# Every fourth raw weight block of the first layer in a fourth buffer, in the room of the third output-map buffer

## The chip, the cores and the metric

The kernel runs on one core of a Trainium2 chip. The metric is the device time of one execution in microseconds (us). Before the change three runs gave a median of 934.77 us (934.74 to 936.48). A core has five engines with queues of their own: TensorE (PE) multiplies matrices into PSUM banks, VectorE (DVE), ScalarE (ACT) and GpSimd (POOL) work elementwise, and SyncE (SP) issues DMA transfers. Each engine takes its instructions in the order in which they were put into its queue; semaphores order the engines against each other.

## The reference

Two layers over a sequence of 512 tokens of width 1024. The first layer projects the normalised input into five parts of 1024 columns; one part feeds a state-space branch, two feed a convolution branch, and two are gates. The second layer is a gated linear attention.

```python
u = rms_norm(x, norm_pre[i])
p = u @ ev_w_in[j]
a_in, a_z, b_val, b_gate, b_z = split(p)          # 1024 columns each
ya = s5_layer(a_in, ...)                          # 64 groups of 16 channels, state of 64
ya = gelu(ya)
ya = ya * sigmoid(ya @ s5_w_glu[j] + s5_b_glu[j]) * silu(a_z)
yb = conformer_conv(b_val, b_gate, ...) * silu(b_z)   # causal width 31, layer norm, projection
y = concatenate([ya, yb]) @ ev_w_out[j]
x = x + rms_norm(y, norm_post[i])
...
# second layer: the same frame around chunked gated linear attention
```

In `s5_layer` every group runs s_t = Lbar s_(t-1) + Bbar u_t and gives y_t = Re(C s_t) + D u_t.

## The kernel before

All products are made in a split precision: a weight block of 128 x 1024 is loaded raw (tile `wraw`), ScalarE rounds it to a high half `wh` (L155), and a low half `wl` = raw - high is made beside it. One output tile of 128 x 512 then takes 24 matmuls: 8 of high weight by high input (L198), 8 of high weight by low input (L199) and 8 of low weight by high input (L201).

The weight blocks form one list in order of use. Blocks 0 to 7 of `ev_w_in` give the input of the state-space branch; blocks 8 to 39 come in eight rounds of four (convolution value, convolution gate, and the two gates); blocks 40 to 47 are `s5_w_glu`; the rest follows. `w_raw` allocates the next raw tile and lets SP issue its load (L118). The tiles rotate through three buffers of one pool on the left side of the on-chip memory. `w_split` makes the halves; for blocks 0 to 47 the low half is made by ACT (L130: minus the raw block, rounded) and a DMA that POOL issues and that adds the raw block to it (L131). So a raw buffer comes free when both L155 and the landing of L131 are done. After each split `w_raw` is called once, so that in the program's order the raw loads run two blocks ahead of the split.

The state-space branch works on eight chunks c of 128 channels, each in three generator functions whose steps are interleaved with the projection blocks:

- `s5_prep(c)` loads the coefficients `cb` (L534; three buffers), makes the input map `bmt`/`bm` (L548, L550, L552 on DVE for the first two chunks, on POOL for the others), the direct kernel `kt` (PE L571 and L575, a copy `ks` on ACT L574, DVE L577), which goes through DRAM into the tile `tm` (L584, L586), and the output map `cme` of 128 x 1024 (the same lines L548, L550, L552, always on DVE, with the scratch tile `pt`). `phases(c)` on POOL (L522 to L524) makes rotation tables that are loaded into `ct` and `st` (L594).
- `s5_in(c)` loads the re-ordered input `u` (L605), multiplies it by `bm` (PE L609), rotates, scans and rotates back (L621 to L636).
- `s5_out(c)` multiplies `u` by `tm` and the states `sv` by `cme` (PE L649), copies and transposes (L653, L658), and applies the gelu into `ya` (ACT L664).

A round c runs `s5_in(c + 1)`, `s5_prep(c + 2)` and `s5_out(c)` in alternating steps and then the four blocks: `value_gate(c)` (sigmoid on ACT L700, product on DVE L701, and the convolution of 31 taps on DVE, L673 to L677, at the lowest priority) and `gate_z` twice (ACT L714, store by SP L715).

The tiles of the state-space branch lie in two pools on the right side, `q5` and `h5`, which are opened after the parameters are computed and closed after the last round; the tiles of the next stage (among them `sz`, `yah`, `yal`, `yfh`, `yfl`) then take this room, each as soon as the tiles that lay there are done with. `cme` has three buffers there, `bm`, `tm` and `kt` two.

The order on each engine isn't written out: a list scheduler puts the instructions into the queues by priority and by the times of its own model, and gives a tile its buffer when one is free in that model. `feed()` raises a priority, `background()` lowers it. A change of a buffer count so can move instructions of any queue.

After round 7 come the GLU product (blocks 40 to 47), the layer norm of the convolution output (`ln`, `xbh`, `xbl`), the output projections, and the second layer.

Of the kernel before, what the change touches and what calls it, by code (L numbers as in the profile page):

```python
# [9 lines left out]
F32 = mybir.dt.float32  # L10
# [7 lines left out]
P = 128  # L18
# [7 lines left out]
GP = 16  # L26
NS = 64
GC = P // GP
NB = 64
DVE_PREP = 2  # L30
TB = S // NB
# [20 lines left out]
def trunk(ctx: ExitStack, tc: tile.TileContext, A: dict, out: bass.AP, dbg: dict | None = None):  # L52
# [6 lines left out]
    wpool = ctx.enter_context(tc.tile_pool(name="wpool", bufs=2, side="left"))  # L59
# [4 lines left out]
    def dump(name, ap):  # L64
        if name in dbg:
            SY.dma_start(dbg[name], ap)
# [3 lines left out]
    def ps(tag="mm"):  # L70
        n = banks["bufs"][tag]
        return banks["pool"].tile([P, S], F32, tag=tag, bufs=n, name=f"ps_{tag}")

    def tmp(shape=(P, S), dt=F32, name="tmp"):
        return t2.tile(list(shape), dt, tag="t2", name=name)
# [35 lines left out]
    wst = {"next_raw": 0, "next_split": 0, "raw": {}, "hl": {}, "low": {}}  # L111

    def w_raw():
        i = wst["next_raw"]
        if i >= len(wlist):
            return
        raw = wpool.tile([P, 1024], F32, tag="wraw", bufs=3, name=f"wraw{i}")
        SY.dma_start(raw, wlist[i][1] if isinstance(wlist[i], tuple) else wlist[i])  # L118
        wst["raw"][i] = raw
        wst["next_raw"] = i + 1  # L120

    def w_low(i, dst=None):


        while wst["next_raw"] <= i:
            w_raw()
        l = wpool.tile([P, 1024], F32R, tag="wl", bufs=3, name=f"wl{i}") if dst is None else dst
        raw = wst["raw"][i]
        with feed():
            SC.activation(l, raw, AF.Copy, scale=-1.0)  # L130
            G.dma_start(l.bitcast(F32), raw, accum_op=ALU.add)  # L131
        wst["low"][i] = l

    def w_split(dst=None):
        i = wst["next_split"]
        while wst["next_raw"] <= i:
            w_raw()
# [4 lines left out]
        if isinstance(wlist[i], tuple):  # L142

            l = wpool.tile([P, 1024], F32R, tag="wl", bufs=3, name=f"wl{i}") if dst is None else dst[1]
            for e in range(2):
                es_, g_ = slice(e * S, (e + 1) * S), wst["gain"][:, 2 * wlist[i][0] + e:2 * wlist[i][0] + e + 1]
                with feed():
                    SC.activation(h[:, es_], raw[:, es_], AF.Copy, scale=g_)  # L148
                    V.scalar_tensor_tensor(out=l[:, es_], in0=raw[:, es_], scalar=g_, in1=h[:, es_].bitcast(F32), op0=ALU.mult, op1=ALU.subtract)  # L149
            wst["hl"][i] = (h, l)  # L150
            wst["next_split"] = i + 1
            w_raw()
            return
# [14 lines left out]
    def feed():  # L168
        return tc.high_priority(offset=1500)
# [310 lines left out]
    q5 = S5.enter_context(tc.tile_pool(name="q5", bufs=1, side="right", reuse_waits="tile"))  # L480
    h5 = S5.enter_context(tc.tile_pool(name="h5", bufs=2, side="right", reuse_waits="tile"))

    dump("u0h", uh.bitcast(F32))


# [21 lines left out]
    def phases(c):  # L507

        sh = [P, GC, 8, 8]
        ws = slice(c // 2 * GC, c // 2 * GC + GC)  # L510

        def w1(w):
            return wb[:, 1, w, ws, :].unsqueeze(3).to_broadcast(sh)

        def w0(w):
            return wb[:, 0, w, ws, :].unsqueeze(2).to_broadcast(sh)

        out_ = []
        for o, (a, b, op) in enumerate(((0, 1, ALU.subtract), (1, 0, ALU.add))):
            r_ = h5.tile(sh, F32, tag=f"ph{o}", bufs=1, name=f"ph{o}_{c}")  # L520
            wt = h5.tile(sh, F32, tag="wt", bufs=1, name=f"wt{o}_{c}")
            G.tensor_tensor(out=r_, in0=w1(0), in1=w0(a), op=ALU.mult)  # L522
            G.tensor_tensor(out=wt, in0=w1(1), in1=w0(b), op=ALU.mult)
            G.tensor_tensor(out=r_, in0=r_, in1=wt, op=op)  # L524
            out_.append(r_.rearrange("p g a b -> p (g a b)"))
        pair[c // 2] = out_
# [3 lines left out]
    def coefficients(c):  # L530

        if c < KT:
            cbs[c] = h5.tile([P, 4, GC, GP], F32, tag="cb", bufs=3, name=f"cb{c}")
            SY.dma_start(cbs[c], A["s5cb"][c])  # L534

    def s5_prep(c):

        g0_ = c * GC
        pe_ = V if c < DVE_PREP else G
        gs = slice(g0_, g0_ + GC)  # L540
        cb = cbs.pop(c)
        cr_ = csps[c % 2]
        SC.activation(cr_[:, :, 0:GP], cb[:, 0], AF.Copy, scale=sgn)

        def outer(eng, o, pt, h, pw, m1, m2, pa):
            sh = list(o.shape)
            hg = slice(g0_ + h * 4, g0_ + h * 4 + 4)
            eng.tensor_tensor(out=o, in0=pw[:, 0, hg, 0:TB].unsqueeze(pa).to_broadcast(sh),  # L548
                              in1=m1.unsqueeze(5 - pa).to_broadcast(sh), op=ALU.mult)
            eng.tensor_tensor(out=pt, in0=pw[:, 1, hg, 0:TB].unsqueeze(pa).to_broadcast(sh),  # L550
                              in1=m2.unsqueeze(5 - pa).to_broadcast(sh), op=ALU.mult)
            eng.tensor_tensor(out=o, in0=o, in1=pt, op=ALU.add)  # L552

        bm = q5.tile([P, GC, P], F32, tag="bm", bufs=2, name=f"bm{c}")
        cme = q5.tile([P, GC, TB, GP], F32, tag="cme", bufs=3, name=f"cme{c}")
        kt = q5.tile([P, GC, GP], F32, tag="kt", bufs=2, name=f"kt{c}")
        for h in range(2):
            hs = slice(h * 4, h * 4 + 4)
            bmt = q5.tile([P, 4, GP, TB], F32, tag="bmt", bufs=2, name=f"bmt{c}")
            pt1 = h5.tile([P, 4, GP, TB], F32, tag="wt", bufs=1, name=f"pt1_{c}")  # L560
            outer(pe_, bmt, pt1, h, prb, cb[:, 2, hs], cb[:, 3, hs], 2)
            tp = ps("aux")
            for j in range(4):
                PE.transpose(tp[:, j * P:(j + 1) * P], bmt[:, j].rearrange("p q s -> p (q s)"), ident)
            with feed():
                SC.copy(bm[:, hs, :], tp.rearrange("p (g n) -> p g n", n=P))
            yield

            kp = ps("aux")
            for j in range(4):  # L570
                PE.matmul(kp[32 * j:32 * j + 32, 0:P], cr_[:, h * 4 + j, :], bmt[:, j].rearrange("p q s -> p (q s)"), start=True, stop=True)  # L571
            ks = q5.tile([P, P], F32, tag="ks", bufs=2, name=f"ks{c}")
            with feed():
                SC.copy(ks, kp[:, 0:P])  # L574
            PE.transpose(kp[:, P:2 * P], ks, ident)  # L575
            with feed():
                V.tensor_tensor(out=kt[:, hs, :], in0=kp[:, P:2 * P].rearrange("p (g q) -> p g q", q=32)[:, :, 0:GP],  # L577
                                in1=dg[:, g0_ + h * 4:g0_ + h * 4 + 4, :], op=ALU.add)
            pt2 = q5.tile([P, 4, TB, GP], F32, tag="pt", bufs=1, name=f"pt2_{c}")
            outer(V, cme[:, hs], pt2, h, pr, cb[:, 0, hs], cb[:, 1, hs], 3)  # L580
            yield
        coefficients(c + 3)
        kd = kt_d[c % 2]
        SY.dma_start(kd[:, 0:TB], kt.rearrange("p g q -> p (g q)"))  # L584
        tm = q5.tile([P, TB, GC, GP], F32, tag="tm", bufs=2, name=f"tm{c}")
        SY.dma_start(tm, bass.AP(tensor=kd.tensor, offset=kd.offset, ap=[[(2 * TB - 1) * P, GP], [P, TB], [1, TB * P]]))  # L586

        if c % 2 == 0:
            phases(c)
        half = slice(c % 2 * NS, c % 2 * NS + NS)  # L590
        ct_, st_ = (h5.tile([P, S], F32, tag=n, bufs=2, name=f"{n}{c}") for n in ("ct", "st"))
        for dst, src in zip((ct_, st_), pair[c // 2]):
            for r_ in range(2):
                SY.dma_start(dst[r_ * NS:r_ * NS + NS], src[half])  # L594
        prep[c] = (bm, cme, tm, ct_, st_)
        yield
# [126 lines left out]
    for c in range(2):  # L723
        run(s5_prep(c), 5)
    run(s5_in(0), 2)
    for c in range(KT):
        nx = s5_in(c + 1) if c + 1 < KT else iter([None] * 2)
        pre = s5_prep(c + 2) if c + 2 < KT else iter([None] * 5)
        cur = s5_out(c)
        run(nx)  # L730
        run(pre, 2)
        run(nx)
        run(cur)
        run(pre, 2)
        run(cur)
        run(pre)
        value_gate(c)
        gate_z(zb_d[c])
        gate_z(za_d[c])
# [127 lines left out]
    for i in range(2):  # L867
        raw = tmp((P, 4, 96))
# [7 lines left out]
    for i in range(2):  # L876
        raw = tmp((96, S))
# [370 lines left out]
```

## Time and profile before

| what | us |
|---|---|
| median of three runs | 934.77 (934.74 to 936.48) |
| the profiled execution, its own time | 936.94 |
| its span from the first to the last instruction | 935.2 |
| PE busy in the span | 895.1 (96%) |
| DVE busy | 645.2 (69%) |
| ACT busy | 485.1 (52%) |
| POOL busy | 225.0 (24%) |

The profile is of one execution on the chip. All later times are us from its first instruction. A row of the view of time order has the start, the duration, the engine (PEld is PE's weight load, SPq a DMA issue by SP), the line of the kernel, the tiles it writes and reads, and in brackets how long the engine had been idle and what ended that. A row of the view of waits has the waiting instruction, what it waited for, the total, the count and the longest. A row of the view of stretches has the busy time of PE, PEld, DVE, ACT and POOL with their counts, then the granted PE clock (1.00 is full), the DMA engines' mean busy share and GB/s.

The stage that the change touches, in stretches of 20 us:

| stretch | PE busy | DVE busy | ACT busy | POOL busy |
|---|---|---|---|---|
| 40 to 60 | 19.93 | 19.86 | 10.23 | 19.30 |
| 60 to 80 | 17.50 | 15.21 | 6.01 | 14.88 |
| 80 to 100 | 18.24 | 11.40 | 15.62 | 15.32 |
| 120 to 140 | 17.97 | 19.25 | 16.95 | 13.10 |
| 140 to 160 | 17.61 | 19.82 | 11.28 | 12.36 |
| 240 to 260 | 19.27 | 17.82 | 15.69 | 2.55 |

### The profile page before, as it was taken

How to read it: one execution, taken by the hardware profiler on the slowest of the kernel's cores; microseconds unless marked ns; L12 is line 12 of the kernel's file. 1: busy time of each engine (PE TensorE's matmuls, PEld its weight loads, DVE VectorE, ACT ScalarE, POOL GpSimd, SP SyncE). 2: the span in 40 equal slices, each digit the busy share in tenths (PEclk: the TensorE clock that was granted, in tenths of full speed). 3: DMA queues.
4: the chain of work that ended last, by engine and by line, in shares of the span. 5: the costliest groups of instructions: out<-in, count | busy, mean ns of one | idle time of the engine just before them, and what ended most of it. 6: DMA issues, size and time to landing. Idle time of an engine off the chain costs nothing. (4 is left out here: it accounts for less than half of the span.)

```text
span 935.2 us, 12132 instructions
## 1 busy us (share of the span) xinstructions
PE 895.1 (96%) x4397; PEld 718.9 (77%) x4397; DVE 645.2 (69%) x1225; ACT 485.1 (52%) x699; POOL 225.0 (24%) x242
## 2 busy tenths in 40 slices
PE   5999998999999999999999979999999999999996
PEld 4876767777788877778887768888888888888885
DVE  7994999999999978822578446694384222744646
ACT  6545686877668745654444654443533243523530
POOL 2795656552041322011054000010000000000022
PEclk9999999999999999999999989999999999999999
DMA  9979987888697894298553122212221223324512
GB/s 288 253 169 228 267 208 181 196 189 203 190 255 203 204 251 135 90 243 186 173 197 113 46 67 96 85 38 77 90 90 68 83 76 136 135 90 152 208 46 90
DMA packets 54820, 142.48 MB, mean 152 GB/s; under 512 B 14245, under 2 KB 15785, under 8 KB 54761
## 3 DMA queue, kind: packets, MB, share of 16 engines
q1 hardware_dynamic: 46696, 112.36, 36.2%
q0 software_dynamic: 8064, 29.36, 17.4%
q8 instruction: 34, 0.56, 0.2%
q14 instruction: 26, 0.20, 0.1%
HBM read 94.92 MB, written 13.22 MB: 116 GB/s over the span
## 5 line engine op out<-in xcount | busy, mean ns | idle before, releaser
L155 ACT CAST wh<-wraw 128x1024 fp32r<-128x1024 f32 x114 | 119.5, 1049 | 138.5 <-PE ps_mm L824 61.9
L676 DVE SCALAR_TENSOR_TENSOR ps_cv<-h,cw,ps_cv 128x512 f32<-128x512 f32 x232 | 161.8, 746 | 2.7 <-ACT ps_cv L673 1.8
L161 DVE TENSOR_TENSOR wl<-wraw,wh 128x1024 fp32r<-128x1024 f32 x58 | 71.6, 1235 | 85.7 <-ACT wh L155 85.7
L198 PE MATMUL ps_mm<-u0h,wh 128*128 128x512 f32 x320 | 128.0, 401 | 1.2 <-ACT tmp L700 0.7
L199 PE MATMUL ps_mm<-u0l,wh 128*128 128x512 f32 x320 | 127.1, 398 | 0.0
L823 PE MATMUL ps_mm<-wh,u1h 128*128 128x512 f32 x240 | 95.6, 400 | 3.3 <-ACT wh L155 3.1
L824 PE MATMUL ps_mm<-wh,u1l 128*128 128x512 f32 x240 | 95.8, 399 | 0.3 <-DVE u1l L206 0.3
L825 PE MATMUL ps_mm<-wl,u1h 128*128 128x512 f32 x240 | 92.6, 402 | 1.7 <-DVE wl L161 1.7
L131 POOL DMA_DIRECT2D wl<-wraw x56 | 48.9, 889 | 172.1 <-ACT wl L130 155.8
L201 PE MATMUL ps_mm<-u0h,wl 128*128 128x512 f32 x320 | 82.4, 396 | 2.2 <-DMA wl<-wraw 2.2
L130 ACT ACTIVATE wl<-wraw 128x1024 fp32r<-128x1024 f32 x56 | 59.2, 1057 | 26.7 <-DMA wraw<-in_w_in_dram 16.2
L198 PEld LDWEIGHTS ps_mm<-u0h,wh 128*128 128x128 f32 x320 | 60.4, 189 | 16.0 <-ACT tmp L700 1.5
L201 PEld LDWEIGHTS ps_mm<-u0h,wl 128*128 128x128 f32 x320 | 59.5, 188 | 16.1 <-DMA wl<-wraw 3.1
L199 PEld LDWEIGHTS ps_mm<-u0l,wh 128*128 128x128 f32 x320 | 60.3, 189 | 13.3 <-issue 0.7
L1092 POOL TENSOR_TENSOR kr<-kr,fac 128x384 f32<-128x384 f32 x8 | 9.1, 1132 | 217.8 <-DVE kr L1088 122.6
L823 PEld LDWEIGHTS ps_mm<-wh,u1h 128*128 128x128 f32 x240 | 45.6, 190 | 14.2 <-ACT wh L155 3.6
L825 PEld LDWEIGHTS ps_mm<-wl,u1h 128*128 128x128 f32 x240 | 45.7, 191 | 13.0 <-DVE wl L161 2.4
L824 PEld LDWEIGHTS ps_mm<-wh,u1l 128*128 128x128 f32 x240 | 45.7, 190 | 11.0 <-DVE u1l L206 0.6
L199 PE MATMUL ps_mm<-u1l,wh 128*128 128x512 f32 x128 | 50.4, 394 | 0.0
L198 PE MATMUL ps_mm<-u1h,wh 128*128 128x512 f32 x128 | 50.3, 393 | 0.0
L149 DVE SCALAR_TENSOR_TENSOR wl<-wraw,ngc,wh 128x512 fp32r<-128x512 f32 x24 | 17.0, 747 | 39.3 <-ACT wh L148 39.3
L903 POOL TENSOR_TENSOR yp<-yp,gain 128x512 f32<-128x512 f32 x8 | 12.6, 1591 | 118.9 <-ACT junk L230 118.9
(348 smaller groups left out, 2041.9 us busy)
## 6 DMA issues: line engine op xcount, KB each, us to landing
wl<-wraw POOLq DMA_DIRECT2D x56, 512.0 KB, 6.4
wraw<-in_w_in_dram SPq DMA_DIRECT2D x40, 512.0 KB, 5.5
wraw<-in_w_out_dram SPq DMA_DIRECT2D x32, 512.0 KB, 3.3
wraw<-in_w_vr_dram SPq DMA_DIRECT2D x32, 512.0 KB, 3.2
wraw<-in_w_qk_dram SPq DMA_DIRECT2D x16, 512.0 KB, 3.2
tm<-kt_d SPq DMA_DIRECT2D x8, 512.0 KB, 7.5
wraw<-in_w_glu_dram SPq DMA_DIRECT2D x8, 512.0 KB, 5.2
wraw<-in_w_pw_dram SPq DMA_DIRECT2D x8, 512.0 KB, 5.3
```

What stands on the lines that cost most here:

```text
L130: SC.activation(l, raw, AF.Copy, scale=-1.0)
L131: G.dma_start(l.bitcast(F32), raw, accum_op=ALU.add)
L149: V.scalar_tensor_tensor(out=l[:, es_], in0=raw[:, es_], scalar=g_, in1=h[:, es_].bitcast(F32), op0=ALU.mult, op1=ALU.subtract)
L155: SC.copy(h, raw)
L161: V.tensor_tensor(out=l, in0=raw, in1=h.bitcast(F32), op=ALU.subtract)
L198: PE.matmul(acc, whv[:, k, :], xh[:, k, :], start=(k == 0), stop=False)
L199: PE.matmul(acc, whv[:, k, :], xl[:, k, :], start=False, stop=False)
L201: PE.matmul(acc, wlv[:, k, :], xh[:, k, :], start=False, stop=(k == KT - 1))
L676: V.scalar_tensor_tensor(out=acc, in0=h[:, k:k + S], scalar=cw[:, c, k:k + 1], in1=acc, op0=ALU.mult, op1=ALU.add)
L823: PE.matmul(accs[tt], xh[:, kt, ts_], whj, start=(first and j == 0), stop=False)
L824: PE.matmul(accs[tt], xl[:, kt, ts_], whj, start=False, stop=False)
L825: PE.matmul(accs[tt], xh[:, kt, ts_], wlj, start=False, stop=(last and j == 1))
```

## The change

The raw blocks 3, 7, 11 and so on up to 35 are allocated in the pool `q5` with a buffer of their own; all others still rotate through the three buffers of the weight pool. A block up to 35 so takes the buffer of the block four before it, where it took that of the block three before. From block 36 on the three buffers rotate as before. The room of the new buffer (4 KB in each partition) is that of the third `cme` buffer, which goes: `cme` has two. The size of the two tiles is the same. The number of loads, and all computation, stay as they are.

```diff
@@ -114,7 +114,11 @@
         i = wst["next_raw"]
         if i >= len(wlist):
             return
-        raw = wpool.tile([P, 1024], F32, tag="wraw", bufs=3, name=f"wraw{i}")
+        if i < 36 and i % 4 == 3:
+
+            raw = wst["pool"].tile([P, 1024], F32, tag="wraw", bufs=1, name=f"wraw{i}")
+        else:
+            raw = wpool.tile([P, 1024], F32, tag="wraw", bufs=3, name=f"wraw{i}")
         SY.dma_start(raw, wlist[i][1] if isinstance(wlist[i], tuple) else wlist[i])
         wst["raw"][i] = raw
         wst["next_raw"] = i + 1
@@ -480,6 +484,7 @@
     q5 = S5.enter_context(tc.tile_pool(name="q5", bufs=1, side="right", reuse_waits="tile"))
     h5 = S5.enter_context(tc.tile_pool(name="h5", bufs=2, side="right", reuse_waits="tile"))
 
+    wst["pool"] = q5
     dump("u0h", uh.bitcast(F32))
@@ -552,7 +557,7 @@
         bm = q5.tile([P, GC, P], F32, tag="bm", bufs=2, name=f"bm{c}")
-        cme = q5.tile([P, GC, TB, GP], F32, tag="cme", bufs=3, name=f"cme{c}")
+        cme = q5.tile([P, GC, TB, GP], F32, tag="cme", bufs=2, name=f"cme{c}")
         kt = q5.tile([P, GC, GP], F32, tag="kt", bufs=2, name=f"kt{c}")
```

## The prediction

> **What bounds the kernel now.** I read the page first, for the busy shares.
>
> ```profile
> PE 895.1 (96%) x4397; PEld 718.9 (77%) x4397; DVE 645.2 (69%) x1225; ACT 485.1 (52%) x699; POOL 225.0 (24%) x242
> ```
>
> PE is busy for 96% of the span, so the time moves only by PE idle time that goes or comes, or by PE running at a lower clock. The change touches only blocks 3 to 35, that is the first 290 us. So the second view is PE's waits from 60 to 340 us (what was waited for: us in total, times, longest):
>
> ```profile
> PE ps_mm L201 <- DMA wl<-wraw: 4.2, 3, 2.0
> PE ps_aux L609 <- DMA u<-u_d: 2.6, 2, 2.4
> PE ps_aux L571 <- DVE kt L577: 2.1, 2, 1.4
> PE ps_aux L575 <- ACT ks L574: 1.8, 1, 1.8
> PE ps_aux L564 <- ACT ya L664: 1.3, 1, 1.3
> PE ps_aux L564 <- DVE kt L577: 0.8, 1, 0.8
> PE ps_mm L198 <- ACT tmp L700: 0.7, 1, 0.7
> ```
>
> Together some 13.5 us, and the change can win no more than this and what hangs on it. No row says that PE waits for a raw block; the low half wl is made on ACT and POOL after the raw block has landed. So the raw blocks matter by a detour: the queue of SP.
>
> ```profile
> SPq L118 <- DMA wl<-wraw: 106.1, 27, 8.9
> SPq L534 <- DVE pt L550: 11.2, 2, 6.0
> ```
>
> From 40 to 300 us SP stood 106.1 us, in 27 waits, before raw-block loads (L118), because the buffer was that of the block three before, whose low half was still being added. SP issues in order: whatever lies behind such a wait leaves late. Which PE waits come from that? I followed two.
>
> The first is at 85 us: rows in order of time of SP, then of ACT, PE and DVE (start, us, engine, line; in brackets the idle time ahead and what ended it):
>
> ```profile
> 61.11 0.33 SPq L118 DMA_DIRECT2D wraw<-in_w_in_dram  x1
> ...
> 70.21 4.89 SPq L594 DMA_DIRECT2D st<-ph  x4
> ...
> 75.83 1.67 SPq L118 DMA_DIRECT2D wraw<-in_w_in_dram  x2
> ```
>
> ```profile
> 82.84 1.06 ACT L130 ACTIVATE wl<-wraw 128x1024 fp32r<-128x1024 f32 x1 [9.08 <-DMA wraw<-in_w_in_dram]
> 85.04 0.33 PE L575 MATMUL ps_aux<-ident,ks 128*128 128x128 f32 x1 [1.76 <-ACT ks L574]
> 87.42 0.69 DVE L701 TENSOR_TENSOR h<-ps_mm,tmp 128x512 f32<-128x512 f32 x1 [9.29 <-ACT tmp L700]
> ```
>
> Raw block 10 leaves at 61.11, block 11 only at 75.83, behind the phase loads. ACT, in order, stands 9.08 us for block 11; behind it stand the copy ks, for which PE waits 1.76 us, and the sigmoid (L700) for which DVE's first convolution waits 9.29 us.
>
> The second is at 142.8 us (PE's and SP's rows, then two rows of the view of stretches):
>
> ```profile
> 131.85 0.39 PE L649 MATMUL ps_aux<-cme,sv 128*64 128x128 f32 x4
> 136.97 0.33 SPq L118 DMA_DIRECT2D wraw<-in_w_in_dram  x1
> ...
> 137.91 0.38 SPq L605 DMA_DIRECT2D u<-u_d  x1
> 142.80 1.86 PE L609 MATMUL ps_aux<-bm,u 128*64 128x128 f32 x16 [2.39 <-DMA u<-u_d]
> ```
>
> ```profile
> 140.00:150.00 10.00, 7.61 (x44) 5.69 (x44) 10.00 (x11) 5.40 (x7) 7.04 (x6) 0.83 0.82 211
> 80.00:90.00 10.00, 8.24 (x53) 5.99 (x52) 1.65 (x4) 7.14 (x12) 5.71 (x7) 1.00 0.82 253
> ```
>
> SP stands until 136.97 for block 20's buffer; the load of u(3) leaves at 137.91, lands 4.9 us later, and PE waits 2.39 us. Then PE's clock shows 0.83 over 140 to 150 us (the column before the last two): 1.7 us more. After the 1.76 us wait at 85 us the clock stayed 1.00.
>
> **The change, part by part.** (1) *Fourth buffer.* Block i now waits for block i-4. For block 11 that is block 7, whose low half had landed when PE took it:
>
> ```profile
> 61.10 2.10 PE L201 MATMUL ps_mm<-u0h,wl 128*128 128x512 f32 x8 [1.17 <-DMA wl<-wraw]
> DMA to landing us min/median/max: 3.2/6.0/11.6
> ```
>
> So block 11 can leave where block 10 does now, at 61.1, ahead of the phase loads, and lands by 72.7 even at the worst time to landing of the raw-block view (0 to 300 us), before ACT is ready for it at 73.76 (82.84 - 9.08). ACT's 9.08 us go. PE's wait doesn't go wholly: the copy ks comes after PE's own matmul, and where ACT is free such a wait is 0.4 us (at 72.50):
>
> ```profile
> 72.50 0.63 PE L564 MATMUL ps_aux<-ident,bmt 128*128 128x128 f32 x4 [0.40 <-ACT ks L574]
> ```
>
> Gain 1.76 - 0.40 = 1.36 us. What is late next for the sigmoid is its own matmuls; I take half of DVE's 9.29 us as won, some 5 us (bounds 0 and 9.29).
>
> Block 20 then waits for block 16, a whole block earlier, instead of block 17. A block is 24 matmuls on PE, 6.3 us by the row at 61.10 (8 in 2.10 us); where the blocks before it kept that distance, its buffer is free at about 130.7 (an estimate: 136.97 - 6.3). Then u(3) waits only for its own buffer, which the read of round 1 frees at 131.85 + 0.39 = 132.24; leaving by 132.3 it lands at 137.2, 3 us before PE comes to it at 140.41. Both parts go: 2.39 + 1.7 = 4.09 us. The issues themselves stay the same in number: 40 raw loads of 0.33 us.
>
> [...]
>
> (2) *Two map buffers instead of three.* The map cme(c) is made by six DVE operations (two each of L548, L550, L552); with two buffers its L548 and L552 wait for the reads of round c-2 instead of c-3.
>
> ```profile
> 50.12 2.34 DVE L548 TENSOR_TENSOR cme<-pr,cb 128x512 f32<-128x512 f32 x3
> 109.28 0.39 PE L649 MATMUL ps_aux<-cme,sv 128*64 128x128 f32 x4
> 113.44 2.57 DVE L548 TENSOR_TENSOR cme<-pr,cb 128x512 f32<-128x512 f32 x2
> L548 DVE TENSOR_TENSOR cme<-pr,cb x16: 677/818/1767, 46.1 to 213.9; 128x512 f32<-128x512 f32 x16
> L552 DVE TENSOR_TENSOR cme<-cme,pt x16: 679/924/1791, 53.1 to 223.2; 128x512 f32<-128x512 f32 x16
> L550 DVE TENSOR_TENSOR pt<-pr,cb x16: 679/786/2137, 49.4 to 220.1; 128x512 f32<-128x512 f32 x16
> ```
>
> Map 2 lies at 50 to 69 us now; it must wait for round 0's reads, which end at 109.67. Map 3 (113.44, 3.8 us after them) moves behind 132.24, and each later map one round, some 23 us (109.67 to 132.24), later. Each is read two rounds, some 45 us, after the reads that free its buffer, and the work takes 5.06 us (2 x (0.818 + 0.924 + 0.786)) spread over some 10 us: nobody waits for a map. Map 3's row shows no idle time of DVE ahead of it, so the wait already now stands among convolution work; I cost the wait itself at nothing, with rival 4 for the cover being gone.
>
> What moves is 5.06 us of DVE time out of a stretch where DVE later idles into one where it is full (10.00 of 10 in the row of 140 to 150). Against it stands the convolution's earlier start, up to 9.29 us, I take about 5. If none of that came, the next to be late would be the normalised map of the second branch:
>
> ```profile
> 402.70 0.69 DVE L206 TENSOR_TENSOR xbl<-ln,xbh 128x512 fp32r<-128x512 f32 x1 [2.35 <-ACT xbh L205]
> 410.29 0.40 PE L199 MATMUL ps_mm<-xbl,wh 128*128 128x512 f32 x1
> ```
>
> Its last piece is ready at 403.39 and read at 410.29: 6.9 us of slack, more than 5.06. Cost 0.
>
> Where map 2 leaves, POOL's operations run beside an idle DVE:
>
> ```profile
> 63.03 1.52 POOL L523 TENSOR_TENSOR wt<-wb 128x512 f32<-128x512 f32 x1
> 64.49 0.88 POOL L131 DMA_DIRECT2D wl<-wraw  x1
> 77.97 1.06 POOL L522 TENSOR_TENSOR ph<-wb 128x512 f32<-128x512 f32 x1 [2.40 <-DMA st<-ph]
> 69.28 0.97 PE L201 MATMUL ps_mm<-u0h,wl 128*128 128x512 f32 x3 [1.02 <-DMA wl<-wraw]
> ```
>
> Two such operations of 1.52 us instead of 1.06 lie just ahead of block 8's addition at 64.49: it can leave 0.9 us earlier, out of PE's wait of 1.02. Bounds 0 and 1.02; I take 0.9, since map 2's last operations lie just there.
>
> (3) *The order of everything.* The schedule is made anew. Waits of PE for kt (L577), behind DVE's queue, are 2.1 + 0.8 = 2.9 us now, and the map's operations now stand elsewhere in that queue. New waits can cost from -2.9 (those go) to +2.9 (as many again); I take one more of the longest, +1.4. Coefficient loads (L534) come later too, behind the later maps; SP stood 11.2 us for two of them, and that stays.
>
> Sum: -1.36 - 4.09 - 0.9 + 1.4 = -4.95 us. Against the profiled span of 935.2 that is 930.3; around the span lie 1.7 us (936.94 for that run). Against the median of 934.77 it is **929.8 us**.
>
> **Rivals.** *1, more goes:* the kt waits shrink and the whole 1.17 and 1.02 at 61 and 69 us go: -4.95 - 1.4 - 1.17 - 0.12 = 927.1. For it: all hang on queues that get emptier. Against: 1.17 is POOL's own backlog.
>
> *2, hidden:* the raw blocks were early enough, and DVE sets the end. [...] The 6.9 us of slack above speaks against it. As a mechanism of this kernel: DVE's earlier start (about 5) and map 2's 5.06 cancel, and PE waits later for what it won: 934.8.
>
> *3, another wait in SP's queue:* coefficient load 6 now waits for map 3, at 137 to 150, exactly ahead of u(3); SP stood up to 6.0 us for such a load. Then only the first gain is left, -1.36 - 0.9 + 1.4: 933.9.
>
> *4, slower:* DVE comes to a map before the reads of round c-2 and stands; behind L548 on DVE stand kt (L577), the evictions L701 and L625, and PE waits for those. Now map 3 starts 3.8 us after the reads; it decides from the point where a round's reads slip by more than that against DVE. One such stand costs PE a wait like that at 142.8, 2.39 + 1.7 = 4.09; in two of the six rounds, 8.2: 938.0.
>
> **How the numbers follow.** Forecast 0.50 (own range 927.5 to 932.5), rival 1 0.08, rival 2 0.12, rival 3 0.12, rival 4 0.18. A measurement here tells about 0.2%, 1.9 us. Faster (below 932.9): forecast and rival 1 but 0.01, 0.57; within: rivals 2 and 3, 0.24; slower 0.19. The range leaves out the faster half of rival 1 and most of rival 4: 927.0 to 937.0.
>
> **What would show it.** Right: no ACT wait of 9 us near 74 to 83 us, the first h (L701) by 83 us, no PE wait for u near 140 us and clock 1.00 there, SP's L118 waits far below 106.1 us. Wrong: DVE idle ahead of L548, a PE wait over 2 us with a clock of 0.83 anywhere from 100 to 290 us, or PE waiting for xbl at 400 us.

## The result, and the profile after: slower by 1.55%

| | before | after |
|---|---|---|
| median, us | 934.75 (934.08 to 936.48, 4 runs) | 949.33 (948.88 to 950.44, 4 runs) |
| ratio | | 1.0155 [1.0137, 1.0172] |
| span of the profiled execution, us | 935.2 | 947.2 |

The forecast of 929.8 us was wrong in sign, and the time lies far outside the range of 927.0 to 937.0. In one experiment below (u's load on ACT's queue in the kernel before) three of the ten runs were far longer than the other seven (992, 1476 and 5007 us, the second at a granted clock of 0.56), and its ratio goes by the seven. The profile page's row of busy times of the kernel after comes first:

```profile
PE 899.0 (95%) x4397; PEld 721.9 (76%) x4397; DVE 649.2 (69%) x1225; ACT 485.1 (51%) x699; POOL 227.7 (24%) x242
```

PE has the same instructions. It is busy for 3.9 us longer (899.0 against 895.1); the other 8.1 of the 12.0 us of span are idle time of PE. The view of PE's waits of the kernel after, 20 to 340 us, names the longest waits (what was waited for: total, times, longest):

```profile
PE ps_mm L202 <- ACT wh L159: 6.4, 1, 6.4
PE ps_mm L205 <- DMA wl<-wraw: 5.4, 1, 5.4
PE ps_aux L614 <- DMA u<-u_d: 4.0, 1, 4.0
PE ps_aux L569 <- DVE bmt L557: 3.7, 1, 3.7
```

(The line numbers of the changed kernel are higher by 4 up to L482 of before and by 5 behind it, so that L118, L131, L155, L198, L201 are L122, L135, L159, L202, L205 now, and L564, L609, L701 are L569, L614, L706.) Three of the four waits are new, all but that for u. They are three single waits, all between 42 and 60 us, by PE's rows in order of time, kernel after:

```profile
42.64 0.80 PE L202 MATMUL ps_mm<-u0h,wh 128*128 128x512 f32 x1 [6.43 <-ACT wh L159]
51.59 0.66 PE L569 MATMUL ps_aux<-ident,bmt 128*128 128x128 f32 x4 [3.67 <-DVE bmt L557]
59.62 3.47 PE L205 MATMUL ps_mm<-u0h,wl 128*128 128x512 f32 x8 [5.37 <-DMA wl<-wraw]
```

The first is the start of weight block 3, the first block in the new buffer. Backwards from it: ACT's row for block 3's raw data, POOL's addition for its low half, and SP's queue, all of the kernel after (start, us, engine, line; in brackets the idle time ahead and what ended it):

```profile
40.60 1.06 ACT L134 ACTIVATE wl<-wraw 128x1024 fp32r<-128x1024 f32 x1 [2.68 <-DMA wraw<-in_w_in_dram]
41.56 1.03 ACT L159 CAST wh<-wraw 128x1024 fp32r<-128x1024 f32 x1
```

```profile
53.53 1.11 POOL L415 TENSOR_TENSOR ya<-wb 128x192 f32<-128x192 f32 x1
54.58 0.87 POOL L135 DMA_DIRECT2D wl<-wraw  x1
```

```profile
7.64 0.33 SPq L122 DMA_DIRECT2D wraw<-in_w_in_dram  x1
...
19.14 9.18 SPq L122 DMA_DIRECT2D wraw<-in_w_in_dram  x3
29.30 2.38 SPq L692 DMA_DIRECT2D u_d<-tmp  x2
34.04 1.00 SPq L610 DMA_DIRECT2D u<-u_d  x2
36.86 0.33 SPq L692 DMA_DIRECT2D u_d<-tmp  x1
37.24 0.42 SPq L122 DMA_DIRECT2D wraw<-in_w_in_dram  x1
```

Which block is which shows in the order of SP's queue, written out with the tile numbers (an excerpt, before on the left):

```
before                              after
wraw3                               wraw4
wraw4                               wraw5
wraw5                               wraw6
store u_d0, load u0, store u_d1     store u_d0, store u_d1, load u0, load u1
wraw6                               store u_d2
load u1, store u_d2                 wraw3
```

So the three loads from 19.14 on are blocks 4, 5 and 6, and block 3 leaves only at 37.24, behind the stores of three finished chunks. In the kernel before the same place of SP's queue held block 3:

```profile
18.05 3.00 SPq L118 DMA_DIRECT2D wraw<-in_w_in_dram  x2
```

That is 19.2 us later (37.24 - 18.05). ACT gets the block at 40.60, PE its high half at 42.64. The addition to the low half leaves only at 54.58, because POOL's queue has it behind the parameter products (L414 to L417), and that is PE's third wait. The second wait is one of PE's own queue: DVE ends the first map at 51.54 us, a little earlier than before (53.17), but PE's queue has the map's transposes at 51.59, where they stood at 63.04 before, so that they now come ahead of blocks 4 to 7. In the view of stretches the two half-idle places have PE's clock at about half as well (busy PE, PEld, DVE, ACT, POOL, then the granted clock):

```profile
38.00:46.00 8.00, 3.36 (x9) 2.72 (x10) 7.97 (x12) 4.84 (x5) 7.61 (x11) 0.57 0.24 85
52.00:63.00 11.00, 5.63 (x17) 3.74 (x16) 10.90 (x8) 0.59 (x1) 10.84 (x12) 0.53 0.73 136
```

The start of a block's first matmul in both traces tells where time was lost and where it came back:

| block | before | after | behind by |
|---|---|---|---|
| 0, low half | 24.74 | 26.66 | 1.9 |
| 3 | 34.12 | 42.64 | 8.5 |
| 5 | 45.11 | 67.75 | 22.6 |
| 16 | 129.38 | 144.11 | 14.7 |
| 18 | 154.67 | 172.24 | 17.6 |
| 36 | 287.45 | 302.18 | 14.7 |
| 47 | 353.44 | 365.31 | 11.9 |

The 22.6 us at block 5 are 15.5 us of waits (6.43 + 3.67 + 5.37), some 4.1 us of half clock (an estimate: 3.36 x 0.43 + 5.63 x 0.47) and 1.9 us that were there at block 0; 1.1 us are left over. (The 1.9 us don't belong to the change: from 15 to 20 us the granted clock was 0.50 in this execution and 1.00 in that of the kernel before, but also 1.00 in that of the experiment with block 3 alone in the new buffer, which loses as much.) From block 5 to block 16 the kernel gets 7.9 us back. PE waits nowhere there, since what it waited for at 61 to 125 us in the kernel before is ready when PE comes 15 to 20 us later; by PE's rows that is 5.9 us of it (1.17 + 1.02 + 0.40 + 1.76 + 0.16 + 1.34). At block 17 it loses 2.9 us again, to the load of u(3). SP's and PE's rows there, kernel after:

```profile
142.68 0.57 SPq L591 DMA_DIRECT2D tm<-kt_d  x1
151.98 0.33 SPq L122 DMA_DIRECT2D wraw<-in_w_in_dram  x1
152.40 0.38 SPq L720 DMA_DIRECT2D za_d<-tmp  x1
152.88 0.38 SPq L610 DMA_DIRECT2D u<-u_d  x1
```

```profile
159.09 0.66 PE L614 MATMUL ps_aux<-bm,u 128*64 128x128 f32 x2 [4.02 <-DMA u<-u_d]
```

By the numbered order the raw load at 151.98 is block 21; in the kernel before it was block 20 that stood ahead of u(3), and 21 stood behind it. SP still stood 8.7 us (143.25 to 151.98), and the wait is longer than before (4.02 against 2.39 us).

### The profile page after: what moved, and what is told of

Same layout as the page of the kernel before. It is cut to its first block, busy times and chain, and to the rows that moved or that the text cites. A ratio compares the mean times of both kernels' runs of the same rounds, so it can differ in the third digit from the quotient of the medians.

```text
span 947.2 us, 12129 instructions
## 1 busy us (share of the span) xinstructions
PE 899.0 (95%) x4397; PEld 721.9 (76%) x4397; DVE 649.2 (69%) x1225; ACT 485.1 (51%) x699; POOL 227.7 (24%) x242
## 3 DMA queue, kind: packets, MB, share of 16 engines
q0 software_dynamic: 8064, 29.36, 17.2%
## 5 line engine op out<-in xcount | busy, mean ns | idle before, releaser
L159 ACT CAST wh<-wraw 128x1024 fp32r<-128x1024 f32 x114 | 119.6, 1050 | 144.8 <-PE ps_mm L203 67.6
L202 PE MATMUL ps_mm<-u0h,wh 128*128 128x512 f32 x320 | 130.8, 410 | 7.2 <-ACT wh L159 6.4
L203 PE MATMUL ps_mm<-u0l,wh 128*128 128x512 f32 x320 | 129.3, 405 | 0.0
L135 POOL DMA_DIRECT2D wl<-wraw x56 | 51.0, 926 | 160.9 <-ACT wl L134 150.4
L205 PE MATMUL ps_mm<-u0h,wl 128*128 128x512 f32 x320 | 83.8, 401 | 5.4 <-DMA wl<-wraw 5.4
L202 PEld LDWEIGHTS ps_mm<-u0h,wh 128*128 128x128 f32 x320 | 62.2, 194 | 23.0 <-ACT wh L159 7.0
L205 PEld LDWEIGHTS ps_mm<-u0h,wl 128*128 128x128 f32 x320 | 60.6, 192 | 20.1 <-DMA wl<-wraw 6.1
L202 PE MATMUL ps_mm<-u1h,wh 128*128 128x512 f32 x128 | 50.3, 393 | 0.0
```

The costliest lines, as they stand in the source:

```text
L159: SC.copy(h, raw)
L202: PE.matmul(acc, whv[:, k, :], xh[:, k, :], start=(k == 0), stop=False)
L203: PE.matmul(acc, whv[:, k, :], xl[:, k, :], start=False, stop=False)
L205: PE.matmul(acc, wlv[:, k, :], xh[:, k, :], start=False, stop=(k == KT - 1))
```

## The experiments

After the result the theories were: **A**, block 3 alone, whose buffer cannot be used, or whose load cannot be queued, while the parameters are computed; **B**, the two map buffers; **C**, the deeper ring's order in SP's queue. The first four runs tell these apart. Each was timed against the kernel before on the same chip, over the same rounds (median 935.5 us, 25 runs). The ratios, with 95% intervals, compare runs of the same rounds and so are not exactly the quotients of the medians.

**Block 3 left in the old ring.**

```diff
-        if i < 36 and i % 4 == 3:
+        if 4 <= i < 36 and i % 4 == 3:
```

> As the changed kernel, but block 3 stays in the weight pool; the fourth buffer begins with block 7. Theory A (the room of the fourth buffer is not free while the parameters are computed, so block 3's load leaves late and PE stands 6.4, 3.7 and 5.4 us at 36 to 60 us): most of the loss goes, 933 to 938 us, no PE wait over 3 us before 60 us. Theory B (two map buffers cost the time): 946 to 950. Theory C (the deeper ring moves loads one block forward in SP's queue all along, and that costs): 944 to 950. A and C agree that PE still waits for u in the third round, since block 21 now stands ahead of it.

932.61 us (930.18 to 935.13), ratio 0.9967 [0.9948, 0.9986]. Of the 14.6 us nothing is left; the kernel is now a little faster than before, just below theory A's 933 to 938. Theory C falls. One wait is new, PE's rows of this run:

```profile
66.20 3.62 PE L205 MATMUL ps_mm<-u0h,wl 128*128 128x512 f32 x8 [3.37 <-DMA wl<-wraw]
```

That is block 7, now the first in the new buffer and late in the same manner (ACT stands 6.21 us for its raw data, to 54.30), at a smaller price.

**Only the two map buffers** (the kernel before, `cme` with `bufs=2`, no fourth raw buffer).

> The kernel before with two map buffers instead of three and nothing else. Theory A: within 2 us of before, 933 to 937. Theory B: 944 to 950. Theory C: as A.

932.46 us (928.62 to 934.97), ratio 0.9966 [0.9949, 0.9984]. Theory B falls, and this half of the change alone gains about 3 us, as much as the versions with an early block 3 in the next runs.

**The fourth buffer in the pool of the phases.**

```diff
-    wst["pool"] = q5
+    wst["pool"] = h5
```

> The changed kernel with the fourth buffer in the other pool of the branch (h5), whose room is free from the start (its coefficient loads leave at 9 us). Theory A: block 3 leaves by 10 us, the startup waits go, 931 to 937. Theory B and theory C: 944 to 950.

932.04 us (928.0 to 934.39), ratio 0.995 [0.993, 0.9971]. Here block 3 is early and the whole ring is four deep. Beside the run with two map buffers alone (932.46) the fourth raw buffer is worth nothing that can be measured. What it did at block 11 shows in ACT's and DVE's rows of this run:

```profile
83.20 1.06 ACT L134 ACTIVATE wl<-wraw 128x1024 fp32r<-128x1024 f32 x1 [1.98 <-DMA wraw<-in_w_in_dram]
```

```profile
81.26 0.69 DVE L706 TENSOR_TENSOR h<-ps_mm,tmp 128x512 f32<-128x512 f32 x1 [3.25 <-ACT tmp L705]
```

ACT's wait of 9.08 us for block 11 is gone (1.98 us are left, for the block behind it), and the first product h comes at 81.26 instead of 87.42. At u(3) nothing is won (SP's and PE's rows of this run):

```profile
138.16 0.33 SPq L122 DMA_DIRECT2D wraw<-in_w_in_dram  x1
139.72 0.39 SPq L610 DMA_DIRECT2D u<-u_d  x1
```

```profile
133.97 0.39 PE L654 MATMUL ps_aux<-cme,sv 128*64 128x128 f32 x4
...
145.14 1.98 PE L614 MATMUL ps_aux<-bm,u 128*64 128x128 f32 x16 [2.90 <-DMA u<-u_d]
```

u's own buffer is free at 134.36 (133.97 + 0.39), but block 21's load stands ahead of u(3) until 138.16.

**Block 3 alone in the new buffer** (all others in the old ring, two map buffers).

```diff
-        if i < 36 and i % 4 == 3:
+        if i == 3:
```

> Only block 3 in the fourth buffer, all others in the ring of three; two map buffers. Theory A: the whole loss is there, 945 to 951, with PE waits of 6.4, 3.7 and 5.4 us ahead of 60 us. Theory B: the same time, but so is the run with two map buffers alone. Theory C: 933 to 938.

949.99 us (948.58 to 952.07), ratio 1.015 [1.0126, 1.0175]: the whole loss, with one load moved. PE's view of waits of this run has the same three rows as the changed kernel, two of them a little different in size:

```profile
PE ps_mm L202 <- ACT wh L159: 6.4, 1, 6.4
PE ps_mm L205 <- DMA wl<-wraw: 4.7, 1, 4.7
...
PE ps_aux L569 <- DVE bmt L557: 4.1, 1, 4.1
```

So theory A holds in its outline: it is block 3. (A fourth raw buffer beside three map buffers was not tried; by the addresses of the tiles 392 bytes of each partition are left free in the kernel before, and the buffer takes 4096.) Two questions were left: why its load is late, and why the second gain, at u(3), did not come. The next four runs (median of before 934.72, 31 runs):

**A pool of its own, opened early.** The fourth buffer's pool is opened before the parameters' pools; the tile, its size and the ring are those of the changed kernel.

```diff
     s5p = S5.enter_context(tc.tile_pool(name="s5p", bufs=1, side="right"))
+    wst["pool"] = S5.enter_context(tc.tile_pool(name="rawp", bufs=1, side="right"))
...
-    wst["pool"] = q5
```

> The changed kernel, with the fourth raw buffer in a pool of its own that is opened before the pools of the parameters instead of in the pool of the maps. Theory A as it now stands (block 3 is late because the pool that holds its buffer opens only after the parameters' pools are closed, so that its load takes a place far behind in SP's queue): block 3 leaves by 20 us, the three PE waits of 6.4, 3.7 and 5.4 us from 42 to 60 us are gone, 932 (931 to 934), as with the buffer in the pool of the phases. Rival: it was the room beside the maps or the number of loads in the ring; then block 3 still lands after 30 us, or it lands early and the time stays above 940.

932.17 us (929.76 to 934.92), ratio 0.9974 [0.9955, 0.9993]. Block 3 leaves with the first loads (SP's rows of this run):

```profile
7.58 1.61 SPq L122 DMA_DIRECT2D wraw<-in_w_in_dram  x2
```

The two loads are blocks 2 and 3. Only the pool was changed, and with it its place in the program and in the memory; the 17.2 us between the two kernels went.

**u's load on ACT's queue, in three kernels.** The load of u (L605, L610) is issued by ACT; first in the kernel before.

```diff
-        SY.dma_start(u, bass.AP(tensor=u_d[c].tensor, ...
+        SC.dma_start(u, bass.AP(tensor=u_d[c].tensor, ...
```

> The kernel before, with one edit: the loads of u (L605) are issued on ACT's queue instead of SP's. Theory Q: PE's wait for u(3) at 142.8 us (2.39 us and 1.7 us of half clock) comes only from the queue, since the load stands on SP behind a raw load that waits for an addition; off that queue the load leaves as soon as its own buffer is free, the wait and the half clock go: 935.5 - 4 = 931.5, and no PE wait for u over 1 us from 100 to 300 us. Rival B: PE would wait there anyway, for the next thing (kt, the maps, the raw block itself), the time lies within 1 us of 935.5 and a wait of PE over 1 us with another name stands near 143. Rival S: ACT, in order, now stands for u's buffer; then ACT shows waits at that line and the time is over 936.5.

935.83 us, ratio 1.0001 [0.9981, 1.002]. Its profile is not read here. Then with two map buffers and no fourth raw buffer:

> The kernel before with two map buffers instead of three and u's loads on ACT's queue: no fourth raw buffer. By theory Q the wait for u of 2.59 us at 121.7 us that two map buffers alone showed goes, with nothing in exchange: 932.5 - 3 = 929.5. By rival B within 1 us of 932.5. By rival S above 933.5, with ACT's waits at the load's line.

932.56 us (927.36 to 936.19), ratio 0.9975 [0.9952, 0.9997]. And with the fourth buffer in the pool of the phases:

> The changed kernel with the fourth raw buffer in the pool of the phases (where block 3 is early) and u's loads on ACT's queue: all that the prediction hoped for, without the raw loads ahead of u. By theory Q the wait for u of 2.90 us at 145 us with its half clock goes: 932 - 4 = 928, and this is the fastest of all. If the fourth raw buffer is worth nothing beside u's own queue: as fast as two map buffers with u on ACT, within 1 us. By rival B within 1 us of 932; by rival S above 933.

931.12 us (929.34 to 933.69), ratio 0.9972 [0.9958, 0.9986]. All three are within about 1.1 us of the same kernel with u on SP's queue (934.7, 932.5 and 932.0, the last two timed in other rounds), where theory Q asked for 3 to 4 us less. Rival B: something else is late next. PE's view of waits of the last of the three says what:

```profile
PE ps_aux L576 <- DVE kt L582: 3.8, 2, 3.1
PE ps_aux L654 <- DMA tm<-kt_d: 1.7, 1, 1.7
```

No wait for u is left, and one for kt has come. The first of the three once more, for a profile (one run):

> The kernel before with u's loads on ACT's queue once more, for its profile, since the profile that was taken of it lies in an execution with a clock of 0.56. Its median was that of the kernel before (ratio 1.0001 [0.9981, 1.002]). Theory N (another thing is next late behind u): the wait for u at 142.8 us is gone and a wait of PE of 1.5 to 3.5 us for kt or for a low half stands within 12 us of it, as with two map buffers (3.08 us for kt at 148.83). Theory S: the wait for u is still there or ACT stands at the load's line. If neither: no PE wait over 1 us from 130 to 165 us, and the gain was lost elsewhere, to be found by the block's starts.

932.45 us. ACT's, PE's and DVE's rows of this run, with three map buffers and the old ring of three:

```profile
133.82 0.37 ACTq L605 DMA_DIRECT2D u<-u_d  x1
```

```profile
151.53 0.43 PE L571 MATMUL ps_aux<-bmt,csp 128*32 128x128 f32 x8 [3.07 <-DVE kt L577]
```

```profile
138.72 2.55 DVE L548 TENSOR_TENSOR cme<-pr,cb 128x512 f32<-128x512 f32 x2
...
146.49 2.13 DVE L550 TENSOR_TENSOR pt<-pr,cb 128x512 f32<-128x512 f32 x1
148.54 1.54 DVE L636 TENSOR_TENSOR sv<-zb,zc 128x504 f32<-128x504 f32 x1
150.00 0.74 DVE L676 SCALAR_TENSOR_TENSOR ps_cv<-h,cw,ps_cv 128x512 f32<-128x512 f32 x1
150.66 0.68 DVE L552 TENSOR_TENSOR cme<-cme,pt 128x512 f32<-128x512 f32 x1
151.27 0.21 DVE L577 TENSOR_TENSOR kt<-ps_aux,dg 128x64 f32<-128x64 f32 x1
```

u leaves at 133.82, four us earlier, and PE stands 3.07 us at 151.53 instead, for the second half of kt(3). That operation is the last in a row of DVE work without a gap, and in this row are map operations that take up to 2.13 us, against 0.68 us for one in the same trace (150.66).

**Map 3 on POOL** (in the kernel with u on ACT and the buffer in the pool of the phases).

```diff
-            outer(V, cme[:, hs], pt2, h, pr, cb[:, 0, hs], cb[:, 1, hs], 3)
+            outer(G if c == 3 else V, cme[:, hs], pt2, h, pr, cb[:, 0, hs], cb[:, 1, hs], 3)
```

> The changed kernel with the fourth raw buffer in the pool of the phases, u's loads on ACT's queue, and the six operations of map 3 alone on POOL instead of DVE. Theory N: once u is early, PE's 3.08 us wait at 149.82 us for the second half of kt(3) comes from map 3, which with two buffers stands just ahead of it on DVE (137 to 149 us); with the map off DVE that wait goes, DVE is behind by 5 us less, and the time is 931.1 - 3 = 928 (926 to 929.5). Rival P: POOL's additions of low halves stand behind the map's operations now, PE waits over 2 us for a low half between 135 and 165 us, and the time is 931 to 934. Rival D: kt(3) is late for what DVE does besides (convolution, rotations); then the wait for kt stays over 2 us and the time within 1 us of 931.1.

934.31 us (933.46 to 935.36), ratio 0.9982 [0.9964, 1.0]. None of the three came as written: the wait for kt is gone, no low half is late, but PE stands 6.16 us for a copy of ACT's at 144.92. Ahead of that copy in ACT's queue is the copy of a scan's result, for which ACT stands 10.57 us. So behind the wait is one row of DVE, and beside that POOL's (PE's, ACT's and DVE's rows, then the first and the last of POOL's from 133 us on):

```profile
144.92 0.79 PE L663 MATMUL ps_aux<-ident,ys 64*128 64x64 f32 x5 [6.16 <-ACT ys L658]
142.41 0.62 ACT L626 COPY zc<-zb 64x512 f32<-64x512 f32 x1 [10.57 <-DVE zb L634]
133.87 8.46 DVE L634 TENSOR_TENSOR_SCAN zb<-rv,za 128x512 f32<-128x512 f32 x1
```

```profile
133.16 2.37 POOL L553 TENSOR_TENSOR cme<-pr,cb 128x512 f32<-128x512 f32 x2
...
139.72 1.52 POOL L557 TENSOR_TENSOR cme<-cme,pt 128x512 f32<-128x512 f32 x1
```

The scan takes 8.46 us; in the kernel before the eight scans take 1.21 to 2.26 us. It ends at 142.33, 1.1 us after the end of the last of POOL's back-to-back operations (139.72 + 1.52 = 141.24). This suggested the last two runs, which take POOL's operations away from beside DVE.

**The transposed maps of groups 2 and 3, then of all groups, on DVE** (same kernel otherwise, map 3 on DVE again).

```diff
-DVE_PREP = 2
+DVE_PREP = 4      # first run; 8 in the second
```

> The changed kernel with the fourth raw buffer in the pool of the phases and u's loads on ACT's queue, and the transposed maps bmt of groups 2 and 3 made on DVE instead of POOL (12 operations). From 130 to 152 us POOL's operations run beside DVE's, and DVE's take 0.9 to 2.6 us there where the same take 0.68 alone; in the kernel with map 3 on POOL one scan took 8.46 instead of 1.21 us beside POOL's. Theory C (DVE is full in that stretch because POOL's operations beside it lengthen its own): DVE's 12 more operations of 0.68 us, 8.2 us, are about paid back by the operations that are lengthened no more; the wait for kt at 149.82 us falls below 1.5 us, and the time is 929 (927.5 to 931). Rival F (DVE is full by its own work): DVE falls behind by some 8 us, the waits for kt grow above 3 us, and the time is 934 or more.

928.09 us (927.59 to 933.49, 5 runs), ratio 0.9939 [0.9908, 0.9971]: the lowest median of all, though with five runs its interval overlaps that of the kernel that it was made from (0.9972 [0.9958, 0.9986]). The wait for kt near 150 us falls from 3.08 to 0.80 us. DVE's rows of this run:

```profile
131.71 1.28 DVE L553 TENSOR_TENSOR cme<-pr,cb 128x512 f32<-128x512 f32 x2
...
145.14 0.21 DVE L582 TENSOR_TENSOR kt<-ps_aux,dg 128x64 f32<-128x64 f32 x1
```

Two map operations took 2.55 us at this place in the trace shown above (138.72, beside POOL); here two take 1.28 us, and kt is done at 145.35. A later map operation in the same row still takes 2.01 us (142.54, beside POOL's phases; POOL is busy for 9.76 of the 10 us from 140 to 150). What is not separated is how much of the gain is shorter operations and how much is that the 12 moved ones stand where DVE had idle time; nor was this edit run in the kernel before, without the fourth buffer and with u on SP's queue.

> As the run before, with the transposed maps of all eight groups on DVE (36 operations moved, 24.5 us at 0.68 us). By theory C DVE's lengthened operations go over the whole branch to 290 us and the time stays below 931. By rival F DVE, which shows no idle time from 140 to 200 us, ends the convolution more than 10 us later, PE waits for kt several times and for the second branch's map xbl at 400 us, and the time is above 938.

937.5 us (935.82 to 939.41), ratio 1.0032 [1.0017, 1.0048]. All waits for kt are gone, and PE's longest wait, 10.46 us, stands where the first layer's second part begins (PE's row of this run):

```profile
406.01 1.22 PE L202 MATMUL ps_mm<-xbh,wh 128*128 128x512 f32 x2 [10.46 <-ACT xbh L209]
```

The time is rival F's, within half a us of its bound, and the mechanism at 400 us is as it says; the waits for kt that it named did not come.

## Why the prediction was wrong, step by step

**The step that failed** is part (3), "The order of everything", with "I take one more of the longest, +1.4". What the runs showed in its place is one load: block 3, the first in the new buffer, takes a place 19.2 us further back in SP's queue, and ACT's, POOL's and PE's queues are put in order with it. The term was put at 1.4 us and measured 22.6 us at block 5, 1.9 of them not its own, and 12.0 us at the end of the span. The text read PE's waits from 60 us on, and what was lost lies ahead of that. Block 3 alone in the buffer loses all of it (1.015), block 3 alone out of it loses nothing (0.9967), and the same buffer in a pool opened early loses nothing (0.9974).

Which pool holds the buffer decides, then: `q5` is late, while `h5`, opened on the next line of the program, is early, and so is the pool of its own. By the addresses of the tiles (bytes of a partition), `q5` (162592 to 212192) lies partly in the room that the parameters' pools had before (182176 to 212192), and `h5` (129824 to 162592) does not; the 4 KB of the new buffer themselves (from 171232) lie in a part of `q5` that no parameter's tile had used. So the buffer's own room was free all the time. That the scheduler's model holds back every tile of a pool until the whole of the pool's room is given back, and so put the load into SP's queue behind three raw loads and five transfers that it took to be ready by then, is argued from these addresses and fits the three runs; no run moved `q5` alone. The prediction knew that the pools are opened after the parameters and that the order comes from the model's times. It applied this to the removed map buffer and not to the first use of the new one. It followed the loads of blocks 11 and 20, in the middle of the stage, and no load from its start.

**Part (1), block 11**: right where block 3 is early. In the run with the buffer in `h5` the wait for ks at 85 us is gone, ACT's 9 us are gone, and h comes at 81.26 (the text asked for 83). The time shows nothing of it beside the maps' own gain (932.04 against 932.46).

**Part (1), block 20**: wrong. "Block 20 then waits for block 16" is so, but "then u(3) waits only for its own buffer" is not: with a ring one deeper the loads move forward by one block in SP's queue, and block 21, which waits for block 17's addition, stands where block 20 stood. A fourth buffer did not take the stand away from SP. And with the stand taken away in another manner (u on ACT's queue) the 4.09 us were not to be had either: kt(3), at the end of a gapless row of DVE work, holds PE 3.07 us some 9 us later. The total of L118's waits, 106.1 us before, shows how little the ring does for SP. The views of SP's waits, 40 to 300 us, first of the kernel after, then of the run with the buffer in `h5`:

```profile
SPq L122 <- DMA wl<-wraw: 92.8, 23, 9.2
```

```profile
SPq L122 <- DMA wl<-wraw: 102.5, 23, 9.4
```

"Far below 106.1" was the sign that would have shown this step right.

On the half clock: the sum's 1.7 us are the granted clock of 0.83 from 140 to 150 us, around a wait of 2.39 us. In these runs the length of a gap alone does not decide whether the clock falls. These are rows of the view of stretches, the first of the run with two map buffers, the second of the run with the buffer in `h5`:

```profile
80.00:90.00 10.00, 7.21 (x49) 5.17 (x48) 1.12 (x2) 6.60 (x11) 5.12 (x6) 1.00 0.75 182
```

```profile
100.00:110.00 10.00, 9.50 (x32) 7.42 (x33) 6.53 (x8) 3.29 (x4) 2.17 (x2) 0.67 1.03 282
```

A gap of 2.79 us in the first (to 85.58) cost no clock (1.00). In the second, a gap of 2.44 us (to 100.50) is followed by matmuls of 128x512 that take 0.63 us, where they take 0.39 us at full clock, and the granted clock is 0.67. What decides was not shown; that the 1.7 us would go with the wait was the author's estimate.

**Part (2)**: right in its parts. The maps alone on two buffers make the kernel faster; in none of the traces read has a map operation idle time of DVE ahead of it, so rival 4 had no place; and the waits near 61 and 69 us fall to 0.44 and 0.69 us from 1.17 and 1.02, a gain of 1.06 where 0.9 was said. That run gains about 2 us more than the 0.9 (935.5 - 932.46 = 3.0). Its trace lacks the wait of 1.98 us at 333 us; there the low half of a block stands on POOL behind a product that waits for a tile from DRAM, and that tile leaves SP 4.1 us earlier (320.05 against 324.18 us). That one causes the other is read from the two traces, not tested.

**The rivals.** None was the case. Rival 3 had the right place (what stands ahead of u(3) in SP's queue) with another transfer. Rival 2's mechanism, DVE setting the pace, is what the traces show in the stretch from 136 to 152 us once u is early, and at 400 us once DVE is given some 24.5 us more (36 operations of 0.68 us).

**The range** held the versions of the change in which block 3 is early (931.1 to 932.6) and not the change itself. Even for those versions the forecast is near by luck: their gain is the maps' (932.46 with the maps alone), where the sum had 5.45 of its us from the fourth buffer and 0.9 from the maps.

## What to carry to other kernels

When a tile moves to another pool, look at its first use: whose room does that pool take over, when is that given back, and what will stand ahead of the first load in its in-order queue by then? A buffer more in a ring does not clear a queue if the loads are queued one block further ahead for it. And before a wait is counted as won, find the next operation that is late: here kt on DVE took 3.07 us of the 4.09 that u's earlier load was to give.

## What the runs showed of the hardware

In one trace (map 3 on POOL) a scan on DVE that takes 1.21 us elsewhere took 8.46 us while POOL ran seven elementwise operations back to back beside it (133.16 to 141.24), and ended 1.1 us after the last of them. In the kernel before, one beside a single such operation (POOL 161.70 to 163.10) took 2.09 us from 162.10 on and also ended 1.1 us after it. What holds DVE up there was not shown. No run tested this by itself.
